# Fronts and backs for the chunks of an SSD layer, with late Tanh in the conv tiles, in a two-layer streaming encoder on one NeuronCore

## The chip, the cores and the metric

One Trainium2 chip, one of its cores. The metric is the device time of one launch, in microseconds, as a median of several runs. Where a profile is read, it is of one execution with its own time.

## The reference

Two layers over 1024 prompt frames of a new stream and 32 sample frames of a running one, width 1024, float32: a Mamba-2 SSD layer, then an HGRN2 layer, each followed by a SwiGLU feed-forward part. The change concerns the SSD layer and the very last norm. Cut to these:

```python
def ssd_mixer(h, conv_buf, ssm_state, in_w, conv_w, conv_b, dt_bias, A_log, D_skip, gnorm_w, out_w):
    proj = h @ in_w                                    # z (2048), xbc (3072), dt (32 heads)
    ...
    for tap in range(SSD_CONV_W):                      # 4 taps
        acc = acc + xpad[:, tap:tap + L].astype(jnp.float32) * conv_w[tap].astype(jnp.float32)
    xbc = jax.nn.silu(acc)                             # x (2048), B and C (4 groups x 128)
    dt = jax.nn.softplus(dt_raw.astype(jnp.float32) + dt_bias.astype(jnp.float32))
    y, S = ssd_scan(xs, dt, A, Bm, Cm, ssm_state.astype(jnp.float32))
    y = y + D_skip.astype(jnp.float32)[:, None] * xs
    yg = y.reshape(Bsz, L, SSD_D_INNER) * jax.nn.silu(z.astype(jnp.float32))
    yg = yg * lax.rsqrt(jnp.mean(yg * yg, axis=-1, keepdims=True) + NORM_EPS)   # per group of 512
    out = yg.astype(h.dtype) @ out_w

# ssd_scan, for each chunk of frames:
        y = jnp.einsum('btsg,btsgh,bsghp->btghp', cb, decay, xdt)               # inside the chunk
        y = y + jnp.einsum('btgn,bghpn->btghp', Cc, S) * jnp.exp(cum)[..., None]  # from the state
        S = jnp.exp(last)[..., None, None] * S + jnp.einsum('bsgh,bsghp,bsgn->bghpn', w_end, xdt, Bc)

# at the end of the trunk
        y = rmsnorm(x, final_norm_w)
```

## The kernel before

Features lie on the 128 partitions, frames on the free axis. The frames are worked in two halves `h`: 512 prompt frames, then 512 prompt frames and the 32 sample frames (544). Every large product is done three times in a reduced fp32 form to keep fp32 accuracy (`product`, lines L346 to L348): the weight `raw` is split by ScalarE into a high part `wh` and by VectorE into a low part `wl` (`wsplit`, recorded under the helper lines L118 and L121), and for each of 8 slices of the contraction TensorE does wh times xh, wh times xl, wl times xh. So the first L348 of a weight can't start before VectorE has made its `wl`. One tile of 128 output features takes 24 matmuls of 512 columns, or twice 24 of 256 or 272.

The SSD layer runs over eight units (half `h`, group `g` of 8 heads). A unit has six conv tiles (C and B and four of x, tile name `ca`; the products of `conv_tile` are evacuated by ScalarE as `pre`, then three taps on VectorE, a Tanh `cth` on ScalarE and a last product on VectorE), four z tiles, and chunks of 128 frames (four, in the second half also one of 32). A chunk (`ssd_chunk`) has small matmuls: scores (L620), four turns of x (L625), a turn of B (L641), the state's part of Y (L648), the new state (L651), and the chunk's own part of Y (L662). `dec`, `xdt`, `xw`, `cbm`, `ec` are made for them on ScalarE and VectorE, from the time steps `dt` (`ssd_dt`), which `ssd_cols` turns once in each half (L543), and from loads of the cumulated steps (`cumB`, `ec`), issued one chunk ahead on SP's queue. After its chunks a unit is gated: Y gets the skip term and z, the squares are summed (`sq`), a matmul adds over partitions (L369), ScalarE makes `rstd` by Ln and Exp with a table load before each, VectorE scales Y in four parts and makes the low parts `yl`. The output products of a unit (`ssd_out`), the z tiles and the next unit's conv tiles are tasks that are spread between chunks: `PRE` = 4 tasks before the first chunk, the rest evenly behind the chunks, and the conv tiles of the next unit behind the gate. In the first unit the second half's input is also squared and turned there (`x_squares`, `x_residual`, L212 and L225).

Each engine runs its own queue in order. Within it, the framework's scheduler sets the rows when the program is built, from what each instruction depends on, from buffers that come free and from where it stands in the program, so a change of the program text moves rows far from the changed lines. PSUM has five banks for products (`mm`) and three for small matmuls and sums (`sc`).

At the end of the program `last_outs` does the last eight output tiles for the first 256 frames. `finish_last` norms these frames: `first` (after tile 5) turns and squares the first four feature tiles, `second` (after tile 7) the other four, then scales and stores.

Of the kernel before, what the change touches and what calls it, by code (L numbers as in the profile page):

```python
# [11 lines left out]
AF = mybir.ActivationFunctionType  # L12
# [4 lines left out]
P = 128  # L17
# [31 lines left out]
def trunk_kernel(ctx, tc, x_prompt, x_sample, state_ssd, cache_conv, state_hgrn,  # L49
# [442 lines left out]
    def ssd_dt(h, xn, blocks, w=None):  # L492
# [4 lines left out]
        e, v, u, ln, t = [T("ys", "dt") for _ in range(5)]  # L497
# [40 lines left out]
    def ssd_cols(h):  # L538
        pk, _, elast = dts[h]
        cols = colt[:, :5 * P].rearrange("p (c t) -> p c t", t=P)  # L540
        for c, (o, n, _) in enumerate(CHUNKS[h]):
            ps = psum_sc()
            PE.transpose(ps[:n, :P], pk[:, o:o + n], ident)  # L543
            V.tensor_copy(cols[:n, c, :], ps[:n, :P])
        dts[h] = cols, elast

# [3 lines left out]
    def conv_tile(h, ct, xn, blocks, w=None):  # L550
# [60 lines left out]
    def ssd_chunk(h, g, c, S, loads, u):  # L611
        o, n, smp = CHUNKS[h][c]
        Bt, Ct, xs, Y = u["x"][0], u["x"][1], u["x"][2:], u["Y"]
        cols, elast = dts[h]
# [4 lines left out]
        ps = psum_sc()  # L619
        PE.matmul(ps[:n, :n], Bx, Cx, start=True, stop=True)  # L620
        cbm = small("cbm")
        tt(cbm[:n, :n], ps[:n, :n], cmask[:n, :n], MUL)
        ps = psum_sc()
        for j in range(4):
            PE.transpose(ps[:n, j * P:(j + 1) * P], xs[j][:, xo:xo + n], ident)  # L625
        x3 = ps[:n, :].rearrange("p (h q) -> p h q", q=64)
        xdt, xw = T("xd", "xdt")[:, :512], T("xd", "xw")[:, :512]
        tt(xdt[:n, :].rearrange("p (h q) -> p h q", q=64), x3,
           cols[:n, c, h0:h0 + 8].unsqueeze(2).to_broadcast([n, 8, 64]), MUL)
        tt(xw[:n, :].rearrange("p (h q) -> p h q", q=64), x3,  # L630
           cols[:n, c, 64 + h0:64 + h0 + 8].unsqueeze(2).to_broadcast([n, 8, 64]), MUL)
# [9 lines left out]
        PE.transpose(ps[:n, :P], Bx, ident)  # L641
# [16 lines left out]
        y1 = psum_sc()
        y13 = y1.rearrange("p (j t) -> p j t", t=P)
        for i in range(8):  # L660
            r = 64 * (i % 2)
            PE.matmul(y13[r:r + 64, i // 2, :n], xdt[:n, i * 64:(i + 1) * 64], cums[i // 4][:n, i % 4, :n],  # L662
                      start=True, stop=True)
        yo = Y[:, :, o:o + n]
        if ec is None:
            act(yo, y13[:, :, :n], AF.Copy)
        else:
            tt(yo, y13[:, :, :n], ec[:, :, :n], ADD)
# [37 lines left out]
    PRE = 4  # L706

# [3 lines left out]
    def ssd_conv_tasks(h, g, u, blocks=None, ws=()):  # L711
        order = [16 + g, 20 + g] + [4 * g + j for j in range(4)]
        ws = dict(zip(order, ws))
        return [lambda ct=ct: u["x"].append(conv_tile(h, ct, xns[h], blocks or BLK[h], ws.get(ct))) for ct in order]

    def ssd_layer(after, ws):
# [13 lines left out]
        for i, (h, g) in enumerate(units):  # L730
# [28 lines left out]
            if g == 0:  # L759
                ssd_cols(h)  # L760
# [645 lines left out]
    def finish_last(groups):  # L1406
# [20 lines left out]
        return first, second  # L1427

    def last_outs(due1, due2):
# [28 lines left out]
        first, second = finish_last(groups_of(h, 0, 256))  # L1458
# [71 lines left out]
```

## Time and profile before

| | |
|---|---|
| median of 3 runs | 2849.74 us (2848.84 to 2850.81) |
| the profiled execution | 2848.86 us, its span 2846.9 us |
| granted TensorE clock, mean | 0.999 |
| TensorE busy | 2824.4 us (99%) |
| VectorE busy | 2131.0 us (75%) |
| ScalarE busy | 1561.8 us (55%) |
| GpSimd busy | 44.5 us (2%) |
| SSD layer in the span | about 0 to 850 us |

Times in the rows are microseconds from the start of the span. In a timeline a row gives start, duration, engine, line, operation, tiles; a duration includes the filling and emptying of the engine, so neighbouring rows overlap, and what an instruction costs its queue is the difference of starts. Square brackets give the idle time of the engine ahead of a row and what ended it. In the chain of work that ended last, a row gives start, duration, line and count.

### The profile page before, as it was taken

The page shows a single profiled execution, that of the slowest core. Times are in us where ns is not written, and L with a number is a line of the kernel's source. Part 1 is how long each engine was busy: PE and PEld are TensorE (multiplying, and loading weights), DVE is VectorE, ACT ScalarE, POOL GpSimd, SP SyncE. Part 2 cuts the span into 40 slices and gives each one's busy share as a digit, 9 for nine tenths or more (in the row PEclk, how much of TensorE's full clock was granted, in tenths as well). Part 3 has the DMA queues.
Part 4 walks back from the last instruction along what each step waited for, and adds up shares of the span by engine and source line. Part 5 has one row for each costly group of instructions (what it writes and reads, how often), then busy time and mean ns, then how long its engine had stood idle before and what let it go on. Part 6 is the DMA issues. An engine that isn't in the chain of part 4 may idle for free.

```text
span 2846.9 us, 48830 instructions
## 1 busy us (share of the span) xinstructions
PE 2824.4 (99%) x19676; PEld 2609.6 (92%) x19676; DVE 2131.0 (75%) x3663; ACT 1561.8 (55%) x2846; POOL 44.5 (2%) x158
## 2 busy tenths in 40 slices
PE   8999999999999999999999999999999999999998
PEld 8777788999989999999999888999989999999998
DVE  7887887787787877797777557655668877787776
ACT  6665554564644654565544666566644554455544
POOL 0000010010000000000000000000000000000000
PEclk9999999999999999999999999999999999999999
DMA  7434344444322432333233222222232333333322
GB/s 190 115 108 115 91 109 105 115 113 106 105 83 88 126 95 91 112 89 105 90 97 105 75 74 74 76 80 80 74 89 91 113 95 92 120 97 104 110 91 69
DMA packets 394516, 281.54 MB, mean 99 GB/s; under 512 B 16289, under 2 KB 382514, under 8 KB 394290
## 3 DMA queue, kind: packets, MB, share of 16 engines
q1 hardware_dynamic: 394274, 278.42, 33.9%
q8 instruction: 154, 2.52, 0.4%
q14 instruction: 72, 0.59, 0.1%
q10 hardware_dynamic: 16, 0.00, 0.0%
HBM read 270.57 MB, written 7.82 MB: 98 GB/s over the span
## 4 chain that ended last, share of the span: by engine, by line
PE 91%; DVE 4%; ACT 2%; DMA 1%; issue 1%; SPq 0%; POOL 0%; DVEq 0%; ACTq 0%; POOLq 0%
PE mm L346 19%; PE mm L347 19%; PE mm L348 19%; PE mm L1177 5%; PE mm L1175 5%; PE mm L1176 5%; PE sc L1177 4%; PE sc L1175 4%; PE sc L1176 4%; PE sc L662 1%; PE sc L651 1%; PE sc L648 1%; PE mm L1451 1%; DVE fixed L121 1%; ACT wh L118 1%
## 5 line engine op out<-in xcount | busy, mean ns | idle before, releaser
L118 ACT ACTIVATE wh<-raw 128x512 fp32r<-128x512 f32 (+1 forms) x687 | 554.8, 816 | 592.0 <-PE mm L347 475.9
L346 PE MATMUL mm<-xn,wh 128*128 128x272 f32 (+2 forms) x1552 | 522.2, 337 | 2.0 <-ACT pre L118 2.0
L348 PE MATMUL mm<-xn,wl 128*128 128x272 f32 (+2 forms) x1552 | 515.9, 333 | 0.9 <-DVE wl L121 0.9
L347 PE MATMUL mm<-xn,wh 128*128 128x272 f32 (+2 forms) x1552 | 515.6, 333 | 0.0
L121 DVE TENSOR_TENSOR wl<-raw,wh 128x1024 fp32r<-128x1024 f32 (+1 forms) x307 | 372.9, 1217 | 144.6 <-ACT wh L118 120.4
L121 DVE TENSOR_TENSOR fixed<-mm,fixed 128x272 f32<-128x272 f32 (+3 forms) x504 | 259.2, 525 | 180.6 <-PE mm L348 173.7
L347 PE MATMUL mm<-fl,wh 128*128 128x272 f32 (+1 forms) x992 | 322.5, 326 | 0.0
L346 PE MATMUL mm<-fh,wh 128*128 128x272 f32 (+1 forms) x992 | 322.5, 326 | 0.0
L348 PE MATMUL mm<-fh,wl 128*128 128x272 f32 (+1 forms) x992 | 322.3, 325 | 0.0
L346 PEld LDWEIGHTS mm<-xn,wh 128*128 128x128 f32 x1552 | 291.4, 188 | 31.9 <-issue 3.0
L348 PEld LDWEIGHTS mm<-xn,wl 128*128 128x128 f32 x1552 | 291.6, 188 | 30.4 <-issue 1.8
L347 PEld LDWEIGHTS mm<-xn,wh 128*128 128x128 f32 x1552 | 291.9, 188 | 27.6 <-issue 1.2
L121 DVE TENSOR_TENSOR wh<-raw,wh 128x512 fp32r<-128x512 f32 x380 | 256.4, 686 | 48.5 <-ACT wh L118 45.9
L1175 PE MATMUL mm<-th,wh 128*128 128x272 f32 (+1 forms) x912 | 261.2, 286 | 0.8 <-ACT s L118 0.8
L1177 PE MATMUL mm<-th,wh 128*128 128x272 f32 (+1 forms) x912 | 260.1, 285 | 0.2 <-DVE wh L121 0.2
L1176 PE MATMUL mm<-tl,wh 128*128 128x272 f32 (+1 forms) x912 | 259.5, 285 | 0.0
L346 PEld LDWEIGHTS mm<-fh,wh 128*128 128x128 f32 x992 | 186.1, 188 | 16.0 <-ACT fh L118 1.6
L348 PEld LDWEIGHTS mm<-fh,wl 128*128 128x128 f32 x992 | 186.6, 188 | 15.4
L347 PEld LDWEIGHTS mm<-fl,wh 128*128 128x128 f32 x992 | 186.5, 188 | 14.9 <-DVE fl L121 0.2
L1175 PEld LDWEIGHTS mm<-th,wh 128*128 128x128 f32 x912 | 171.7, 188 | 2.9 <-ACT s L118 2.2
L1175 PE MATMUL sc<-xn,wh 128*128 128x272 f32 (+1 forms) x608 | 172.9, 284 | 0.5 <-ACT wh L118 0.5
L1177 PE MATMUL sc<-xn,wh 128*128 128x272 f32 (+1 forms) x608 | 173.0, 285 | 0.0
(313 smaller groups left out, 6648.8 us busy)
## 6 DMA issues: line engine op xcount, KB each, us to landing
raw<-in_ffn_w_gate_dram SPq DMA_DIRECT2D x88, 512.0 KB, 3.8
raw<-in_ffn_w_up_dram SPq DMA_DIRECT2D x88, 512.0 KB, 4.4
raw<-in_ffn_w_down_dram SPq DMA_DIRECT2D x88, 512.0 KB, 3.9
raw<-in_ssd_in_w_dram SPq DMA_DIRECT2D x80, 512.0 KB, 4.1
raw<-in_hgrn_in_w_dram SPq DMA_DIRECT2D x64, 512.0 KB, 4.3
cumB<-cumd SPq DMA_DIRECT2D x64, 256.0 KB, 4.2
raw<-in_ssd_out_w_dram SPq DMA_DIRECT2D x32, 512.0 KB, 3.5
raw<-in_hgrn_out_w_dram SPq DMA_DIRECT2D x16, 512.0 KB, 3.5
```

Of the source, the lines that this page charges most:

```text
L118: keep(A.activation(out=out, in_=in_, func=f, **kw))
L121: keep((eng or V).tensor_tensor(out=out, in0=a, in1=b, op=op))
L346: PE.matmul(ps[:, :bn], a, mh, start=(k == 0), stop=False)
L347: PE.matmul(ps[:, :bn], a, ml, start=False, stop=False)
L348: PE.matmul(ps[:, :bn], b, mh, start=False, stop=(k == n - 1))
L648: PE.matmul(y23[:, j, :n], S[:, j * P:(j + 1) * P], Cx, start=True, stop=True)
L651: PE.matmul(pp, Btok[:n, :], xw[:n, :], start=True, stop=True)
L662: PE.matmul(y13[r:r + 64, i // 2, :n], xdt[:n, i * 64:(i + 1) * 64], cums[i // 4][:n, i % 4, :n], start=True, stop=True)
L1175: PE.matmul(ps[:, :n], a, mh, start=(k == 0 and not more), stop=False, skip_group_check=True)
L1176: PE.matmul(ps[:, :n], a, ml, start=False, stop=False, skip_group_check=True)
L1177: PE.matmul(ps[:, :n], b, mh, start=False, stop=(k == 3), skip_group_check=True)
L1451: PE.matmul(ps[:, :bn], a, x[:, b0:b0 + bn], start=i == 0, stop=i == len(ts_) - 1)
```

## The change

1. `ssd_chunk` is cut into `ssd_front` (scores, the turns of B and x, and what is made of them: `cbm`, `Btok`, `xdt`, `xw`, `dec`) and `ssd_back` (the state's part of Y, the new state, the chunk's part of Y). The loop issues the back of chunk c-1, the front of chunk c, the loads of chunk c+1, then the tasks. A front takes two `mm` banks instead of `sc` banks. `LEAD` = 3 tasks stand before the first front, where `PRE` = 4 stood before the first chunk.
2. `ssd_cols` goes; the fronts of group 0 turn the time steps of their chunk themselves. One `dt` tile moves to another buffer.
3. A conv tile's Tanh and last product (`conv_silu`) are issued after the taps of the next conv tile; the last two after the last tile.
4. At the end of the program three of the four last feature tiles are turned and squared after tile 6 (`most`), the fourth after tile 7.

```diff
-        e, v, u, ln, t = [T("ys", "dt") for _ in range(5)]
+        e, v, u, ln, t = [T(k, "dt") for k in ("s", "ys", "ys", "ys", "ys")]
...
-    def ssd_cols(h):
-        pk, _, elast = dts[h]
-        cols = colt[:, :5 * P].rearrange("p (c t) -> p c t", t=P)
-        for c, (o, n, _) in enumerate(CHUNKS[h]):
-            ps = psum_sc()
-            PE.transpose(ps[:n, :P], pk[:, o:o + n], ident)
-            V.tensor_copy(cols[:n, c, :], ps[:n, :P])
-        dts[h] = cols, elast
...
+        return a, W
+
+    def conv_silu(a, W):
         th = T("w", "cth")
         act(th[:, :W], a[:, :W], AF.Tanh)
         stt(a[:, :W], th[:, :W], 1.0, a[:, :W], ADD, MUL)
-        return a
...
-    def ssd_chunk(h, g, c, S, loads, u):
+    def ssd_front(h, g, c, loads, u):
...
+        ps, px = psum_mm(), psum_mm()
         PE.matmul(ps[:n, :n], Bx, Cx, start=True, stop=True)
+        PE.transpose(ps[:n, P:2 * P], Bx, ident)
+        if not g:
+            PE.transpose(ps[:n, 2 * P:3 * P], pk[:, o:o + n], ident)
+            V.tensor_copy(cols[:n, c, :], ps[:n, 2 * P:3 * P])
+        for j in range(4):
+            PE.transpose(px[:n, j * P:(j + 1) * P], xs[j][:, xo:xo + n], ident)
+        cbm, Btok = small("cbm"), small("Btok")
         tt(cbm[:n, :n], ps[:n, :n], cmask[:n, :n], MUL)
+        act(Btok[:n, :], ps[:n, P:2 * P], AF.Copy)
...
+        return decs, ec, xdt, xw, Btok, Cx
+
+    def ssd_back(h, g, c, S, made, u):
...
         if ec is not None:
+            y2 = psum_sc().rearrange(quads, t=P)
             for j in range(4):
+                PE.matmul(y2[:, j, :n], S[:, j * P:(j + 1) * P], Cx, start=True, stop=True)
+            tt(ec[:, :, :n], y2[:, :, :n], ec[:, :, :n], MUL)
+            S3 = S.rearrange("p (h q) -> p h q", q=64)
+            tt(S3, S3, elast[:, h0:h0 + 8, c:c + 1].to_broadcast([P, 8, 64]), MUL)
+        pp, y1 = psum_sc(), psum_sc().rearrange(quads, t=P)
         PE.matmul(pp, Btok[:n, :], xw[:n, :], start=True, stop=True)
+        for i in range(8):
+            r = 64 * (i % 2)
+            PE.matmul(y1[r:r + 64, i // 2, :n], xdt[:n, i * 64:(i + 1) * 64], decs[i // 4][:n, i % 4, :n],
+                      start=True, stop=True)
...
+    LEAD = 3
...
+        made = []
+
+        def task(i, ct):
+            made.append(conv_tile(h, ct, xns[h], blocks or BLK[h], ws.get(ct)))
+            u["x"].append(made[-1][0])
+            for m in made[-2:-1] if i + 1 < len(order) else made[-2:]:
+                conv_silu(*m)
...
-            for t in tasks[:PRE]:
-                t()
-            tasks = tasks[PRE:]
-            for c, (o, n, smp) in enumerate(CHUNKS[h]):
-                nxt = chunk_loads(h, g, c + 1, False) if c + 1 < nch else None
-                ssd_chunk(h, g, c, Ss if smp else Sst[g], loads, u)
-                loads = nxt
-                q = -(-len(tasks) // (nch - c))
...
+            run(tasks[:LEAD])
+            tasks = tasks[LEAD:]
+            made = None
+            for c in range(nch + 1):
+                if c:
+                    ssd_back(h, g, c - 1, Ss if CHUNKS[h][c - 1][2] else Sst[g], made, u)
+                if c < nch:
+                    made = ssd_front(h, g, c, loads, u)
+                if c + 1 < nch:
+                    loads = chunk_loads(h, g, c + 1, False)
+                if c < nch:
+                    q = -(-len(tasks) // (nch - c))
+                    run(tasks[:q])
+                    tasks = tasks[q:]
...
+        def most():
+            for g, ss in zip(groups, sums):
+                ps, yo = psum_sc(), T("w", "yo")[:, :512]
+                turned(g, ps, range(3))
+                squared(ps, yo, 0, 384, ss[:, 1:2])
+                tt(ss[:, 0:1], ss[:, 0:1], ss[:, 1:2], ADD)
+                last.append((ps, yo))
+
         def second():
-            last = [finish_half(g, 1, ss, psum_sc, "w") for g, ss in zip(groups, sums)]
+            for g, (ps, yo) in zip(groups, last):
+                turned(g, ps, (3,))
+            for ss, (ps, yo) in zip(sums, last):
+                squared(ps, yo, 384, 512, ss[:, 1:2])
...
-        mid[5] = first
+        mid[5], mid[6] = first, most
```

How this moves rows in the queues, at three places. The numbers in names differ between the two programs.

VectorE in the first unit's conv tiles, where `wl_642` (now `wl_639`) is the low part of the fifth conv tile's weight. Before, rows 70 to 77:

```order
L121 TENSOR_TENSOR dt_361<-dt_361,dt_358 128x512
L124 SCALAR_TENSOR_TENSOR ca_350<-cth_355,ca_350 128x512
L121 TENSOR_TENSOR dt_359<-dt_359,dt_361 128x512
L121 TENSOR_TENSOR wl_642<-raw_639,wh_641 128x1024
L513 TENSOR_SCALAR dt_360<-dt_359,fixed 128x512
L517 COPY dt_358<-dt_359 32x512
L514 SCALAR_TENSOR_TENSOR dt_362<-fixed,dt_360 128x512
L124 SCALAR_TENSOR_TENSOR ca_493<-pre_438,fixed,ca_493 128x512
```

Now, rows 78 to 88, the end of rows 69 to 88:

```order
L124 SCALAR_TENSOR_TENSOR ca_350<-cth_495,ca_350 128x512
L518 COPY dt_355<-dt_359 32x512
L121 TENSOR_TENSOR dt_355<-dt_359 32x512
L528 COPY fixed<-dt_355 32x4
L124 SCALAR_TENSOR_TENSOR ca_559<-pre_504,fixed,ca_559 128x512
L124 SCALAR_TENSOR_TENSOR ca_490<-cth_564,ca_490 128x512
L121 TENSOR_TENSOR dt_355<-dt_355,dt_356 32x512
L124 SCALAR_TENSOR_TENSOR ca_559<-pre_504,fixed,ca_559 128x512
L121 TENSOR_TENSOR wl_639<-raw_636,wh_638 128x1024
L124 SCALAR_TENSOR_TENSOR ca_559<-pre_504,fixed,ca_559 128x512
L121 TENSOR_TENSOR wl_708<-raw_705,wh_707 128x1024
```

The weight moved from row 73 to row 86, behind the scan (L514, row 77 now) and the taps and last products of the tiles `ca_490` and `ca_559`.

VectorE at the first unit's gate, where the last sum of squares releases L369, and `wl_1404` (now `wl_1393`) is the low part of the weight of the next unit's fourth conv tile. Before, rows 169 to 177:

```order
L121 TENSOR_TENSOR sq_1188<-sq_1188,sq_1196 128x512
L124 SCALAR_TENSOR_TENSOR ca_1259<-pre_1230,fixed,ca_1259 128x512
L121 TENSOR_TENSOR wl_1404<-raw_1401,wh_1403 128x1024
L121 TENSOR_TENSOR wl_1463<-raw_1460,wh_1462 128x1024
L124 SCALAR_TENSOR_TENSOR ca_1259<-cth_1264,ca_1259 128x512
L124 SCALAR_TENSOR_TENSOR Y_801<-Y_801,fixed,rstd_1199 128x512 x3
L121 TENSOR_TENSOR yl_1206<-Y_801,yh_1205 128x512
L124 SCALAR_TENSOR_TENSOR Y_801<-Y_801,fixed,rstd_1199 128x512
L121 TENSOR_TENSOR yl_1211<-Y_801,yh_1210 128x512
```

Now, the sum of squares is row 173; rows 180 to 191:

```order
L225 COPY fixed<-sc_1319 128x4x128
L124 SCALAR_TENSOR_TENSOR Y_789<-Y_789,fixed,rstd_1191 128x512 x3
L121 TENSOR_TENSOR yl_1198<-Y_789,yh_1197 128x512
L124 SCALAR_TENSOR_TENSOR Y_789<-Y_789,fixed,rstd_1191 128x512
L121 TENSOR_TENSOR yl_1203<-Y_789,yh_1202 128x512
L124 SCALAR_TENSOR_TENSOR ca_1366<-pre_1337,fixed,ca_1366 128x512
L121 TENSOR_TENSOR yl_1208<-Y_789,yh_1207 128x512
L225 COPY fixed<-sc_1378 128x4x128
L121 TENSOR_TENSOR yl_1213<-Y_789,yh_1212 128x512
L121 TENSOR_TENSOR wl_1393<-raw_1390,wh_1392 128x1024
L124 SCALAR_TENSOR_TENSOR ca_1366<-cth_1430,ca_1366 128x512
L225 COPY fixed<-sc_1437 128x4x128
```

The weight moved behind the four scalings of Y and the four low parts `yl`.

TensorE at the same place. Before, from the last product ahead of L369:

```order
L347 MATMUL mm_1409<-xn,wh_1403 128x512
L369 MATMUL sc_1200<-sq_1188,fixed 128x512
L212 MATMUL sc_1271<-fixed 128x128 x4
L212 MATMUL sc_1277<-fixed 128x128 x4
L348 MATMUL mm_1409<-xn,wl_1404 128x512
L346 MATMUL mm_1409<-xn,wh_1403 128x512
```

Now:

```order
L347 MATMUL mm_1398<-xn,wh_1392 128x512
L369 MATMUL sc_1192<-sq_1180,fixed 128x512
L212 MATMUL sc_1260<-fixed 128x128 x4
L212 MATMUL sc_1266<-fixed 128x128 x4
L212 MATMUL sc_1319<-fixed 128x128 x4
L212 MATMUL sc_1325<-fixed 128x128 x4
L212 MATMUL sc_1378<-fixed 128x128 x4
L212 MATMUL sc_1384<-fixed 128x128 x4
L212 MATMUL sc_1437<-fixed 128x128 x4
L212 MATMUL sc_1443<-fixed 128x128 x4
L212 MATMUL sc_1496<-fixed,xrow_785 128x32 x4
L348 MATMUL mm_1398<-xn,wl_1393 128x512
```

All the turns of the second half's input, 36 with x4 in each row, moved in front of the L348 that needs the weight.

VectorE at the joint of the halves, where `wl_4031` (now `wl_4008`) belongs to the fourth conv tile of the second half's first unit. Before, from the scaling of Y:

```order
L124 SCALAR_TENSOR_TENSOR Y_3140<-Y_3140,fixed,rstd_3787 128x512
L121 TENSOR_TENSOR dt_3686<-dt_3686,dt_3690 128x544
L124 SCALAR_TENSOR_TENSOR ca_3876<-pre_3818,fixed,ca_3876 128x547
L121 TENSOR_TENSOR dt_3689<-dt_3689,dt_3686 128x544
L124 SCALAR_TENSOR_TENSOR ca_3876<-pre_3818,fixed,ca_3876 128x547
L121 TENSOR_TENSOR dt_3687<-dt_3687,dt_3689 128x544
L124 SCALAR_TENSOR_TENSOR ca_3876<-pre_3818,fixed,ca_3876 128x547
L121 TENSOR_TENSOR yl_3799<-Y_3140,yh_3798 128x512
L513 TENSOR_SCALAR dt_3688<-dt_3687,fixed 128x544
L517 COPY dt_3686<-dt_3687 32x544
L514 SCALAR_TENSOR_TENSOR dt_3690<-fixed,dt_3688 128x544
L121 TENSOR_TENSOR wl_4031<-raw_4028,wh_4030 128x1024
```

Now, the scaling starts at row 498; rows 503 to 514:

```order
L121 TENSOR_TENSOR yl_3784<-Y_3124,yh_3783 128x512
L121 TENSOR_TENSOR dt_3646<-dt_3650 32x512
L121 TENSOR_TENSOR dt_3646<-dt_3650 32x32
L528 COPY fixed<-dt_3646 32x4
L530 COPY fixed<-dt_3646 32x1
L124 SCALAR_TENSOR_TENSOR ca_3856<-pre_3798,fixed,ca_3856 128x547
L124 SCALAR_TENSOR_TENSOR ca_3925<-pre_3867,fixed,ca_3925 128x547
L121 TENSOR_TENSOR dt_3646<-dt_3646,dt_3647 32x544
L124 SCALAR_TENSOR_TENSOR ca_3856<-pre_3798,fixed,ca_3856 128x547
L121 TENSOR_TENSOR yl_3789<-Y_3124,yh_3788 128x512
L124 SCALAR_TENSOR_TENSOR ca_3925<-pre_3867,fixed,ca_3925 128x547
L121 TENSOR_TENSOR wl_4008<-raw_4005,wh_4007 128x1024
```

Counted from the first scaling as the first, the weight moved from row 14 to row 17, behind all of the `dt` chain and taps of two conv tiles; and on TensorE 146 products stand between the last chunk's L658 (before L662) and the L348 that needs it, where 187 stood.

More of the change, by code (lines that the diff above doesn't have):

```diff
@@ L618, in ssd_chunk @@
         cums, ec = loads
-        ps = psum_sc()
+        ps, px = psum_mm(), psum_mm()
         PE.matmul(ps[:n, :n], Bx, Cx, start=True, stop=True)
-        cbm = small("cbm")
+        PE.transpose(ps[:n, P:2 * P], Bx, ident)
[5 more added lines that the diff above has]
+        cbm, Btok = small("cbm"), small("Btok")
         tt(cbm[:n, :n], ps[:n, :n], cmask[:n, :n], MUL)
[L623 to L626, printed above, removed]
+        act(Btok[:n, :], ps[:n, P:2 * P], AF.Copy)
+        x3 = px[:n, :].rearrange("p (h q) -> p h q", q=64)
         xdt, xw = T("xd", "xdt")[:, :512], T("xd", "xw")[:, :512]
[L628 to L631, printed above, removed]
+        for t, k in ((xdt, 0), (xw, 64)):
+            tt(t[:n, :].rearrange("p (h q) -> p h q", q=64), x3,
+               cols[:n, c, k + h0:k + h0 + 8].unsqueeze(2).to_broadcast([n, 8, 64]), MUL)
+        decs = []
         for q in range(2):
@@ L644, in ssd_chunk @@
+    @lifted("chunk")
+    def ssd_back(h, g, c, S, made, u):
+        o, n, smp = CHUNKS[h][c]
+        decs, ec, xdt, xw, Btok, Cx = made
+        elast = dts[h][2]
+        h0 = g * 8
+        quads = "p (j t) -> p j t"
         if ec is not None:
-            y2 = psum_sc()
-            y23 = y2.rearrange("p (j t) -> p j t", t=P)
+            y2 = psum_sc().rearrange(quads, t=P)
             for j in range(4):
-                PE.matmul(y23[:, j, :n], S[:, j * P:(j + 1) * P], Cx, start=True, stop=True)
@@ L657, in ssd_chunk @@
             tt(S, S, pp, ADD)
[L658 to L668, printed above, removed]
+            tt(yo, y1[:, :, :n], ec[:, :, :n], ADD)
@@ L713, in ssd_conv_tasks @@
         ws = dict(zip(order, ws))
-        return [lambda ct=ct: u["x"].append(conv_tile(h, ct, xns[h], blocks or BLK[h], ws.get(ct))) for ct in order]
+        made = []
[4 more added lines that the diff above has]
+                conv_silu(*m)
+        return [lambda i=i, ct=ct: task(i, ct) for i, ct in enumerate(order)]
     def ssd_layer(after, ws):
@@ L1426, in second @@
                 finish_out(g, 1, yo)
-        return first, second
+        return first, most, second
     def last_outs(due1, due2):
@@ L1457, in last_outs @@
                 out(m, [g], 256, LEN[h] - 256)
-        first, second = finish_last(groups_of(h, 0, 256))
+        first, most, second = finish_last(groups_of(h, 0, 256))
         later = groups_of(h, 256, LEN[h])
         mid = {m: lambda g=g: finish(g) for m, g in zip((0, 2, 4), later)}
-        mid[5] = first
+        mid[5], mid[6] = first, most
         for m in range(KD):
```

27 lines of the change are left out of this document (12 added, 15 removed).

## The prediction

> **What bounds the kernel now.** I read the page's busy shares first, then the table of TensorE's waits, then the stretches around each of them.
>
> ```profile
> PE 2824.4 (99%) x19676; PEld 2609.6 (92%) x19676; DVE 2131.0 (75%) x3663; ACT 1561.8 (55%) x2846; POOL 44.5 (2%) x158
> ...
> PE mm L212 <- DMA fixed<-in_x_prompt_dram: 3.9, 1, 3.9
> PE mm L346 <- ACT pre L118: 2.0, 2, 1.5
> ...
> PE mm L348 <- DVE wl L121: 0.9, 1, 0.9
> PE sc L543 <- ACT pre L118: 0.9, 2, 0.5
> ...
> PE sc L369 <- DVE sq L121: 0.5, 1, 0.5
> ...
> 460.00:800.00 340.00, 340.00 (x2761) 321.97 (x2760) 270.93 (x439) 194.71 (x426) 19.34 (x70) 1.00 0.42 106
> ```
>
> TensorE is busy for 99% of the span. In the waits (total us, how often, longest) the SSD layer has only 2.0 + 0.9 + 0.9 + 0.5 = 4.3 us; the 3.9 is the first load and stays. The last row is a stretch of 340 us in the second half's units (columns: length, then PE, PEld, DVE, ACT, POOL busy): PE 340.00 of 340.00, DVE 271, ACT 195. So a reordering that keeps the same matmuls can win about 4.3 us, while anything that holds TensorE's queue is added in full. The question is where VectorE's new order hands TensorE an operand late.
>
> **The change, part by part.** Everything is set against the profiled execution: span 2846.9, time 2848.86, which is 0.9 us under the median of 2849.74.
>
> *Grouping of small matmuls.* As many as before: the turns of `cols` move into the fronts, the rest only stands closer together.
>
> ```profile
> 95.84 0.60 PE L625 MATMUL sc<-fixed,ca 128*128 128x128 f32 x4
> 96.20 0.48 PE L347 MATMUL mm<-xn,wh 128*128 128x512 f32 x1
> 96.52 0.27 PE L641 MATMUL sc<-fixed,ca 128*128 128x128 f32 x1
> ...
> 115.77 1.10 PE L369 MATMUL sc<-sq,fixed 128*128 128x512 f32 x2 [0.47 <-DVE sq L121]
> 116.70 1.04 PE L212 MATMUL sc<-fixed 128*128 128x128 f32 x8
> 117.50 0.48 PE L348 MATMUL mm<-xn,wl 128*128 128x512 f32 x1
> ...
> 2826.01 2.83 PE mm L1451 x24
> ```
>
> Costs are differences of starts. The last row, from the chain, gives 24 products of 256 columns in 2.83 us: 0.118 each, so 0.236 at 512 columns and 0.125 at 272. Four small ones take 0.36 us and the product behind them 0.32 instead of 0.236, 0.45 in all; eight take 0.80 and about the same exit, 0.89. Two groups of four cost what one of eight costs: grouping gives 0, within 1 us over the 36 chunks.
>
> *Steady units.* Between a front and its back stand 24 products of 512 columns or 48 of 272, 5.7 or 6.0 us, beside the rest of the chunk's matmuls; VectorE and ScalarE have room by the 340 us row. The loads of the next chunk now go behind the front on SP's queue:
>
> ```profile
> cumB<-cumd SPq DMA_DIRECT2D x64, 256.0 KB, 4.2
> ```
>
> They land 4.2 us after issue, less than those products. POOL only keeps its few memsets and carries. I take 0 here. If the cover were missing in one chunk in six, it would cost under 1 us each.
>
> *Start (30 to 64 us).* The deferred Tanh no longer stands ahead of an evacuation, which should remove this wait and one of L543:
>
> ```profile
> 39.64 1.42 DVE L121 TENSOR_TENSOR dt<-dt,dt 128x512 f32<-128x512 f32 x2 [0.74 <-ACT dt L118]
> 42.18 1.22 DVE L121 TENSOR_TENSOR wl<-raw,wh 128x1024 fp32r<-128x1024 f32 x1
> 44.05 1.21 DVE L514 TENSOR_TENSOR_SCAN dt<-fixed,dt 128x512 f32<-128x512 f32 x1
> 45.18 0.72 DVE L124 SCALAR_TENSOR_TENSOR ca<-pre,fixed,ca 128x512 f32<-128x512 f32 x1
> ...
> 51.94 0.39 PE L346 MATMUL mm<-xn,wh 128*128 128x256 f32 x1 [1.53 <-ACT pre L118]
> ```
>
> But in the new VectorE order the low part of the fifth conv tile's weight (`wl_639`) is row 86, not 73 (`wl_642`, the row at 42.18). Ahead of it stand the `dt` chain and the taps of three tiles. Row 69 waits for ScalarE's `dt`, 39.64 before; two evacuations now stand ahead of that on ScalarE, so about 41.15. Rows 69 to 86: the scan 1.13, the weight 1.13, seven tap and Tanh products at 0.66, five tensor operations at 0.6 to 0.7 and four copies and scalings at 0.2 to 0.45: 11.5 us. So `wl_639` is ready at about 52.6. TensorE reaches that tile 24 products before the wait above (50.2 - 2.8 = 47.4) and has six products that don't need it, 0.7 us. It stands 4.5 us, in two pieces; 1.53 + 0.42 go. Net **+2.5** (bounds -2, the waits gone and nothing new, and +4.5).
>
> *The first unit's gate.* Below are VectorE's and ScalarE's rows after the sum of squares that L369 waits for:
>
> ```profile
> 116.20 2.35 DVE L121 TENSOR_TENSOR wl<-raw,wh 128x1024 fp32r<-128x1024 f32 x2
> 119.91 0.69 DVE L124 SCALAR_TENSOR_TENSOR ca<-cth,ca 128x512 f32<-128x512 f32 x1 [1.35 <-ACT cth L118]
> 120.52 2.07 DVE L124 SCALAR_TENSOR_TENSOR Y<-Y,fixed,rstd 128x512 f32<-128x512 f32 x3
> 122.51 0.68 DVE L121 TENSOR_TENSOR yl<-Y,yh 128x512 fp32r<-128x512 f32 x1
> 123.11 0.74 DVE L124 SCALAR_TENSOR_TENSOR Y<-Y,fixed,rstd 128x512 f32<-128x512 f32 x1
> ...
> 117.25 0.69 ACT L118 ACTIVATE rstd<-sc,fixed 128x512 f32<-128x512 f32 x1
> 117.96 1.28 ACT L118 ACT_TABLE_LOAD   x1
> ```
>
> Before, the two weights at 116.20 come ahead of the scaling of Y, and TensorE always has conv products. Now `wl_1393` is row 189, behind all four scalings and all four `yl`. Let D be the end of the sum (row 173). ScalarE: a tap to wait for 0.66, Tanh 0.52 (a little less than Ln), a table load 1.28, Ln 0.7, a copy 0.5, a table load 1.28, Exp 0.55: scaling starts at D + 5.5. VectorE from there: four scalings and a tap at 0.66, four `yl` and a copy at 0.6, the weight at 1.17: 7.5, so D + 13.1 with the latencies. TensorE after D has L369 (0.24) and the 36 transposes of L212 at 0.10 to 0.11, held back a little by their banks: done at D + 5.0. Its next row is the L348 that needs `wl_1393`. It stands **8.1 us**. Fewer products are also left ahead of L369 than VectorE's gate takes; it waits 1.35 instead of 0.47: **+0.9**.
>
> *The joint of the halves.* The same happens to the fourth conv tile's `wl_4008` (before `wl_4031`):
>
> ```profile
> 384.93 0.69 DVE L121 TENSOR_TENSOR Y<-sc,ec 128x512 f32<-128x512 f32 x1
> ...
> 386.13 1.41 DVE L124 SCALAR_TENSOR_TENSOR Y<-ca,fixed,Y 128x512 f32<-128x512 f32 x2
> ...
> 391.19 0.69 DVE L121 TENSOR_TENSOR sq<-sq,sq 128x512 f32<-128x512 f32 x1
> ...
> 399.25 2.08 DVE L124 SCALAR_TENSOR_TENSOR Y<-Y,fixed,rstd 128x512 f32<-128x512 f32 x3 [2.10 <-ACT rstd L118]
> ...
> 409.08 1.19 DVE L121 TENSOR_TENSOR wl<-raw,wh 128x1024 fp32r<-128x1024 f32 x1
> ...
> 409.14 0.29 PE L347 MATMUL mm<-xn,wh 128*128 128x272 f32 x1
> 410.32 0.40 PE L348 MATMUL mm<-xn,wl 128*128 128x272 f32 x1 [0.90 <-DVE wl L121]
> ```
>
> Let S be the start of the last chunk's Y (384.93). Before, the weight was done at S + 25.3, and TensorE needed it at S + 24.3. Now VectorE has one weight (1.15), the gate (386.13 to 391.19, 5.06), the square sums and half the `dt` chain until S + 13.4, waits for `rstd` until S + 14.9 (L369 after 93 products of 0.125 at S + 11.6, then Ln, a table load, Exp), and has 11.4 us of rows up to `wl_4008`: S + 26.3. TensorE now has only 146 products plus L369 and four transposes behind S: it comes at S + 19.0. It stands 7.3 us. The waits of this stretch before go: the 0.90 above, and the second waits in the rows of `pre` and of L543, 2.0 - 1.5 and 0.9 - 0.4: 1.9. Net **+5.4** (bounds -1.9 and +7.3). At the six other joints the same count leaves TensorE served; the nearest has 0.3 us to spare.
>
> *The end.* Six of the eight last transposes move ahead of the last four matmuls and delay them by 0.65 us, where five were hidden; the two last squares shrink from 512 to 128 columns.
>
> ```profile
> 2838.57 0.86 PE sc L1380 x6
> ...
> 2839.45 1.27 ACT yo L118 x4
> ```
>
> Of the 0.86 some 0.65 merely moves, of the 1.27 about 0.4 goes: **+0.25** (bounds -0.4, +0.65).
>
> *The clock after a stall.* TensorE stands for longer than 3 us nowhere after the first load until its work is over. There:
>
> ```profile
> 3.00:4.00 1.00, 0.09 (x1) 0.12 (x2) 0.00 (x0) 0.20 (x1) 0.00 (x0) 1.00 0.98 281
> ...
> 2841.00:2842.00 1.00, 0.00 (x0) 0.00 (x0) 0.90 (x3) 0.85 (x2) 0.00 (x0) 1.00 0.00 0
> 2842.00:2843.00 1.00, 0.00 (x0) 0.00 (x0) 0.77 (x2) 0.72 (x1) 0.00 (x0) 0.73 0.28 104
> 2843.00:2844.00 1.00, 0.00 (x0) 0.00 (x0) 0.00 (x0) 0.00 (x0) 0.00 (x0) 0.50 1.03 393
> ```
>
> The clock granted is the third figure from the end: the last transposes end at about 2839.6, and from 2842.5 it is 0.50. After some 3 us of rest TensorE gets half its clock. How long it stays low under work no row shows; at least 0, and the longest seen is the 4.4 us to the end of the span, which would lose 2.2. I take 3 us, as long as the fall needed, so 1.5 lost, at each of the two long stalls: **+3.0** (0 to 4.4).
>
> [...]
>
> **Sum:** 2.5 + 8.1 + 0.9 + 5.4 + 0.25 + 3.0 = 20.15 us. 2848.86 + 20.15 = 2869.0, with the 0.9 to the median **2870**.
>
> **Rivals.** *The clock does not fall at the stalls* (they come in pieces, or the gate is slower under load): 2867. For it speaks the row at 3 to 4 us, where TensorE has rested 3.9 us since the start and the clock is 1.00.
>
> *The lateness is absorbed*: TensorE comes to the two places later than my count has it, because other waits or products stand before them, and VectorE is on time; the start's +2.5 and the waits that go then cancel: 2850, give or take 4. Against it: both stalls are counted from S and D, so what happens before these does not shift them. It would take 7 to 8 us of VectorE's rows to vanish.
>
> *Faster*: the deferred Tanh and the fronts remove the 4.3 us of waits in the table and cause none; at best another 1 us from grouping: 2849.7 - 5.3 = 2844.5. Its place is 50 to 62 us and 409 to 430 us, and it decides if `wl_1393` comes before D + 5.0 and `wl_4008` before S + 19.0. The 340 us row shows that nothing else is left to win.
>
> **How the numbers follow.** Stalls with the falling clock 0.50 (2870, own range 2862 to 2876), stalls without it 0.28 (2867), absorbed 0.16 (2850), faster 0.06 (2844.5). A measurement of this kernel can tell about 0.2%, 5.7 us, from no change, so slower means above 2855.4: both stall cases and the upper edge of the third, 0.80; within it 0.14; faster 0.06. The range leaves out the fast case and the lower half of the absorbed one, 0.14 together: from 2850; upwards it takes in the upper bounds of the start (2.0 more), the joint (1.9), the clock (1.4) and the end (0.4): 2870 + 5.7 = 2876.
>
> **What would show it.** In the changed kernel's waits a row of L348 on VectorE's `wl` with some 15 us in two or three waits, near 124 to 132 and near 420; a granted clock below 1.00 behind them; no L346 wait on `pre` above 1 us; the last matmul half a microsecond nearer to the end. I am wrong if those `wl` rows are short, or if the steady units show waits of TensorE.

## The result, and the profile after

The changed kernel takes 2871.86 us (median of 6 runs, 2871.07 to 2872.36), the kernel before 2849.85 beside it: a ratio of 1.0078, 95% interval [1.0068, 1.0089], 22.0 us more. 2870 was forecast. The profiled execution of the changed kernel took 2872.36 us, with a span of 2870.6 against 2846.9, so the traces differ by 23.7. Its mean granted clock is 0.995 (0.999 before).

From the page after, the span and the busy times, and then TensorE's waits (total us, how often, longest):

```profile
span 2870.6 us, 48888 instructions
...
PE 2828.4 (99%) x19676; PEld 2615.3 (91%) x19676; DVE 2125.9 (74%) x3665; ACT 1569.1 (55%) x2852; POOL 106.5 (4%) x158
```

```profile
PE mm L348 <- DVE wl L121: 17.6, 3, 8.3
...
PE mm L346 <- ACT wh L118: 3.0, 1, 3.0
PE mm L346 <- DVE fixed L121: 2.5, 3, 1.5
...
PE sc L369 <- DVE sq L121: 1.1, 1, 1.1
```

The number of matmuls is the same. The waits on `pre` and of the turned time steps are gone, and three waits for a weight's low part, 17.6 us in all, stand in their place. TensorE's timeline shows where (start, duration, line, and in brackets the idle time ahead):

```profile
52.31 0.38 PE L346 MATMUL mm<-xn,wh 128*128 128x256 f32 x1 [2.99 <-ACT wh L118]
...
54.38 0.58 PE L348 MATMUL mm<-xn,wl 128*128 128x256 f32 x1 [1.52 <-DVE wl L121]
54.76 0.41 PE L346 MATMUL mm<-xn,wh 128*128 128x256 f32 x1
54.97 0.41 PE L347 MATMUL mm<-xn,wh 128*128 128x256 f32 x1
...
123.94 1.13 PE L369 MATMUL sc<-sq,fixed 128*128 128x512 f32 x2 [1.10 <-DVE sq L121]
124.90 3.66 PE L212 MATMUL sc<-fixed 128*128 128x128 f32 x32
128.49 0.43 PE L212 MATMUL sc<-fixed,xrow 32*128 32x32 f32 x4
137.26 0.80 PE L348 MATMUL mm<-xn,wl 128*128 128x512 f32 x1 [8.35 <-DVE wl L121]
...
141.56 0.39 PE L346 MATMUL mm<-xn,wh 128*128 128x512 f32 x1
...
426.66 0.60 PE L778 MATMUL sc<-fixed,sr 128*128 128x128 f32 x4
435.00 0.59 PE L348 MATMUL mm<-xn,wl 128*128 128x272 f32 x1 [7.74 <-DVE wl L121]
...
438.47 0.29 PE L348 MATMUL mm<-xn,wl 128*128 128x272 f32 x1
```

VectorE's timeline gives the other side, the last sum of squares and the weight at the first gate, then the same at the joint of the halves:

```profile
123.20 0.68 DVE L121 TENSOR_TENSOR sq<-sq,sq 128x512 f32<-128x512 f32 x1
...
129.67 2.08 DVE L124 SCALAR_TENSOR_TENSOR Y<-Y,fixed,rstd 128x512 f32<-128x512 f32 x3 [1.40 <-ACT rstd L118]
...
136.00 1.22 DVE L121 TENSOR_TENSOR wl<-raw,wh 128x1024 fp32r<-128x1024 f32 x1
...
408.71 0.68 DVE L121 TENSOR_TENSOR Y<-sc,ec 128x512 f32<-128x512 f32 x1
...
433.73 1.22 DVE L121 TENSOR_TENSOR wl<-raw,wh 128x1024 fp32r<-128x1024 f32 x1
```

In both places VectorE works on, apart from its wait for `rstd`; the weight is simply the last of a long run of rows, while TensorE has run out of rows that can do without it.

In the stretches (length; PE, PEld, DVE, ACT, POOL busy; granted clock third from the end) the clock is at half behind all three:

```profile
53.00:59.00 6.00, 4.62 (x21) 4.62 (x22) 6.00 (x8) 1.54 (x2) 0.10 (x1) 0.50 0.92 242
...
132.00:141.00 9.00, 3.73 (x9) 2.96 (x10) 9.00 (x15) 6.24 (x12) 0.00 (x0) 0.50 0.20 63
...
432.00:438.00 6.00, 3.00 (x13) 3.00 (x14) 6.00 (x8) 4.57 (x8) 4.19 (x3) 0.50 0.80 199
...
455.00:850.00 395.00, 394.94 (x3071) 368.25 (x3070) 306.48 (x497) 218.25 (x472) 59.70 (x75) 1.00 0.40 107
```

The last row is the whole second half of the SSD layer behind the joint: TensorE rests for 0.06 us in 395, at full clock.

**Where the 23.7 us of span are.** The new waits are 17.6 + 3.0 + 1.1 = 21.7 in the table; the ones that went were 4.3, so 17.4. Counted as differences of starts it is 17.2. The clock: from 137.26 to 141.56 ten products took 4.30 us, 2.31 at their usual 0.231; from 435.00 to 438.47 fifteen took 3.47 instead of 1.88; and at the start twenty products at 0.213 instead of 0.118, with the edges, lost 2.2. Together 2.0 + 1.6 + 2.2 = 5.8. The rows without a wait, with the grouping of the small matmuls, gave back about 2.2. The wait at the entry of the first feed-forward part (the row of `fixed`, longest 1.5, before 0.5) costs 1.0, the end 0.5, and the first product starts at 15.94 instead of 14.53, 1.4 later. That makes 23.7.

### The profile page after: what moved, and what is told of

It reads as the page before. It is cut to its first block, busy times and chain, and to the rows that moved or that the text cites. A ratio compares the mean times of both kernels' runs of the same rounds, so it can differ in the third digit from the quotient of the medians.

```text
span 2870.6 us, 48888 instructions
## 1 busy us (share of the span) xinstructions
PE 2828.4 (99%) x19676; PEld 2615.3 (91%) x19676; DVE 2125.9 (74%) x3665; ACT 1569.1 (55%) x2852; POOL 106.5 (4%) x158
## 4 chain that ended last, share of the span: by engine, by line
PE 89%; DVE 5%; ACT 3%; DMA 1%; issue 1%; SPq 0%; POOL 0%; ACTq 0%; DVEq 0%; POOLq 0%
PE mm L346 19%; PE mm L348 19%; PE mm L347 19%; PE mm L1186 4%; PE mm L1184 4%; PE mm L1185 4%; PE sc L1186 3%; PE sc L1184 3%; PE sc L1185 3%; PE sc L658 1%; PE sc L655 1%; DMA raw<-in_ffn_w_up_dram 1%; DVE wh L121 1%; PE sc L650 1%; DVE fixed L121 1%
## 5 line engine op out<-in xcount | busy, mean ns | idle before, releaser
L348 PE MATMUL mm<-xn,wl 128*128 128x272 f32 (+2 forms) x1552 | 518.8, 335 | 17.7 <-DVE wl L121 17.6
L121 DVE TENSOR_TENSOR fixed<-mm,fixed 128x272 f32<-128x272 f32 (+3 forms) x540 | 268.7, 507 | 190.3 <-PE mm L348 181.0
L348 PEld LDWEIGHTS mm<-xn,wl 128*128 128x128 f32 x1552 | 293.5, 189 | 48.9 <-DVE wl L121 19.4
L348 PE MATMUL mm<-fh,wl 128*128 128x272 f32 (+1 forms) x992 | 322.8, 326 | 0.0
L348 PEld LDWEIGHTS mm<-fh,wl 128*128 128x128 f32 x992 | 186.6, 188 | 15.3
L347 PEld LDWEIGHTS mm<-fl,wh 128*128 128x128 f32 x992 | 186.6, 188 | 14.9 <-DVE fl L121 0.2
```

The source lines that it names most:

```text
L121: keep((eng or V).tensor_tensor(out=out, in0=a, in1=b, op=op))
L347: PE.matmul(ps[:, :bn], a, ml, start=False, stop=False)
L348: PE.matmul(ps[:, :bn], b, mh, start=False, stop=(k == n - 1))
```

## The experiments

My theory was that the whole loss comes from the third part, the deferred Tanh and last product: VectorE's rows are reordered by it, so that three weight splits come late, and the rests let the clock fall. The rival was that the fronts and backs bring the loss with them, because they need other banks and rows. "Ratio" is against the kernel before, timed beside it.

**Tanh at once** (label silu_at_once): all of the change but its third part.

```diff
-            for m in made[-2:-1] if i + 1 < len(order) else made[-2:]:
-                conv_silu(*m)
+            conv_silu(*made[-1])
```

> The changed kernel with its third part undone: each conv tile's Tanh and last product follow its own taps again; fronts, backs, the turned time steps and the new end stay. In its order the fifth conv tile's weight of the start is back at row 73, the first gate's weight stands again ahead of the scaling of Y, and at the joint of the halves the weight comes some 3.9 us late (7.0 by the same count in the changed kernel). Theory (late weights): the start costs nothing more than before, the first unit 1.3 us (L369 0.65, weight 0.7), the joint 3.9 + about 1.6 for a low clock - 2.8 for waits that are gone, grouping -1.7, the end +0.5: 2849.85 + 2.8 = about 2852.5 us (2850 to 2855). Rival (the cut into fronts and backs and its banks cost the time themselves): above 2865 us.

It took 2850.76, before 2850.20: ratio 1.0003 [0.9994, 1.0012]. Against the kernel before beside it, the changed kernel lost 22.0 us and this one 0.6, so some 21 of the 22 us come from the order of two instructions for each conv tile; by the interval of this run it is 19 to 24. Its stretch at the start, and the one wait on a weight that is left:

```profile
30.00:64.00 34.00, 34.00 (x275) 33.22 (x274) 27.83 (x45) 21.85 (x36) 1.63 (x10) 1.00 0.56 137
```

```profile
PE mm L348 <- DVE wl L121: 3.8, 1, 3.8
```

The stall at the joint is only halved, so the fronts and backs have a part in that one, and win about as much elsewhere. No kernel was run with the third part alone, so it stays open whether the late Tanh would cost the same in the old order.

**Deferral at the start only, and everywhere else only** (late_start, late_rest):

```diff
+            late = blocks is not None          # late_rest: blocks is None
-            for m in made[-2:-1] if i + 1 < len(order) else made[-2:]:
+            for m in (made[-2:-1] if i + 1 < len(order) else made[-2:]) if late else made[-1:]:
                 conv_silu(*m)
```

> The changed kernel with the deferred Tanh kept in the six conv tiles of the start alone; all later conv tiles have Tanh and last product behind their own taps. Theory (each place of a late weight pays for itself): the start's stalls of 3.1 and 1.7 us and some 2.4 us of low clock come back on top of silu_at_once (2850.8), less the nothing that stands there now: about 2858 us (2855.5 to 2859.5). Rival (the start's stall is absorbed by VectorE's slack in the first chunks): 2851 us.

> The complement: Tanh and last product follow their own taps in the start's six tiles, and are deferred in all later units. Theory: the stall of 8.4 us at the first gate, the 7.9 us at the joint and their low clock stay, the start's 7 us go: about 2865 us (2863 to 2867). Together with late_start the two parts make up the whole way from silu_at_once to the changed kernel, 21 us. Rival (the gate's stall comes from VectorE having fallen behind in the start): below 2860 us.

They took 2857.80 and 2863.26, before 2849.54: ratios 1.0027 [1.0017, 1.0038] and 1.0047 [1.0035, 1.0060]. Against the kernel before beside each, and less the 0.6 of silu_at_once, that is 7.7 and 13.2 us; together 20.9 of the 21.4 that lie between silu_at_once and the changed kernel. The rival of late_rest, that the gate's stall comes from VectorE having fallen behind in the start, is refuted by the 8.35 that stay there. The places add up: late_rest has two waits, 16.1 us, on the weights of the gate and the joint (8.35 and 7.78), late_start the start's 2.99 and 1.27 beside a wait of 3.83 at the joint, the one that stays with the Tanh at once. Of the 7.7 that the start costs, the stall is 4.3 and the clock 2.2.

TensorE's waits in late_start, then in late_rest:

```profile
PE mm L348 <- DVE wl L121: 5.1, 2, 3.8
...
PE mm L346 <- ACT wh L118: 3.0, 1, 3.0
```

```profile
PE mm L348 <- DVE wl L121: 16.1, 2, 8.3
```

**Weights lifted** (weights_lifted): everything as in the changed kernel, but three splits get a priority: those of the late weights of the gate and the joint, and of one more weight behind the gate. The late weight of the start gets none. In the built program the rows of three engines change around these two places, not the three splits alone.

```diff
-        w = w or wsplit(conv_w_unit(ct), KD)
+        if w is None:
+            raw = conv_w_unit(ct)
+            with tc.high_priority(100) if (h, ct) in ((0, 5), (0, 7), (1, 1)) else nullcontext():
+                w = wsplit(raw, KD)
```

> The changed kernel with all its parts; only the weight splits of three conv tiles (two in the second unit, one in the first of the second half) are given 100 rows of priority. By its order the first gate's weight is in time and the joint's 3.7 us late; the start keeps its late weight. Theory (late weights): the 8.4 us stall and its 2.0 us of low clock go, at the joint 4 us go; 2871.9 - 14.5 = about 2857 us (2854 to 2860). Rival (the deferred Tanh itself makes VectorE or ScalarE later, the weight's row is only where it shows): the stall moves to the next row and the time stays above 2866 us.

```profile
PE mm L348 <- DVE wl L121: 5.6, 3, 4.2
```

2857.82: ratio 1.0026 [1.0017, 1.0035]. The gate's stall of 8.35 is gone and the joint's 7.74 is 4.18; the start is as it was. 14 of the 22 us are won back by a priority on three splits, with the Tanh still late. This shows the mechanism for the gate and the joint: not the Tanh itself is late for anyone, but what the scheduler puts ahead of a weight because of it. For the start, only the deferral itself was taken away and put back (late_rest, late_start).

**Joint lifted** (joint_lifted): Tanh at once, and the joint's weight with priority 160.

```diff
+            with tc.high_priority(160) if (h, ct) == (1, 1) else nullcontext():
+                w = wsplit(raw, KD)
...
-                conv_silu(*m)
+            conv_silu(*made[-1])
```

> As silu_at_once, and at the joint of the halves the fourth conv tile's weight split is given 160 rows of priority, so that its low part stands ahead of the work on Y and dt. Theory (late weights): the joint's stall and its low clock go, 5.5 us less than silu_at_once: about 2847 us (2845 to 2849), 0 to 5 us faster than the kernel before. Rival (the joint is held by the dt chain or by the loads, not by this weight): within 1 us of silu_at_once.

It took 2849.77, ratio 0.9999 [0.9991, 1.0008]: within what a measurement can tell from no change, and the gain that I expected missed. It came within 1 us of silu_at_once, as the rival had it. The wait moved to another engine. TensorE's rows, then ScalarE's:

```profile
410.46 0.60 PE L780 MATMUL sc<-fixed,sr 128*128 128x128 f32 x4
413.11 0.59 PE L346 MATMUL mm<-xn,wh 128*128 128x272 f32 x1 [2.06 <-ACT Ss L118]
413.50 0.43 PE L347 MATMUL mm<-xn,wh 128*128 128x272 f32 x1
...
416.63 0.29 PE L346 MATMUL mm<-xn,wh 128*128 128x272 f32 x1
```

```profile
410.84 0.65 ACT L118 ACTIVATE dt<-dt 32x544 f32<-32x544 f32 x1 [1.94 <-DVE dt L121]
411.52 1.06 ACT L118 ACTIVATE wh<-raw 128x1024 fp32r<-128x1024 f32 x1
412.48 0.58 ACT L118 ACTIVATE Ss<-sc 128x512 f32<-128x512 f32 x1
```

The copy of the turned state `Ss` stands on ScalarE behind a row of `dt` that VectorE feeds late, and behind the weight's high part. And behind a rest of only 2.06 us the granted clock was 0.50 from 414 to 416, with products 0.227 apart instead of 0.125, until about 416.6. In the same execution the mean granted clock was also 0.83 from 490 to 500 and from 900 to 910, where it was 1.00 in that of silu_at_once: by the means 3.4 us at half clock in each. So the profiled execution kept little of the shorter stall.

**Pause filled, and joint kept busy.** Does the rest itself bring the clock down, or the stall's place? Two kernels give TensorE products whose result nobody uses, behind the four turns at the joint: 8 of 512 columns in joint_lifted (pause_filled), 24 in the changed kernel (joint_kept_busy). If the rest does, pause_filled keeps a clock of 1.00 there and ends 1.6 us earlier than joint_lifted (2849.8), at about 2848.

```diff
+                if i == 4:
+                    wm = psum_sc()
+                    for _ in range(8):
+                        PE.matmul(wm[:, :512], onesr, xns[1][0][0][:, :512], start=True, stop=True)
```

> joint_lifted with 8 products added that serve nothing (512 columns, 1.9 us), which stand right behind the four state turns, where joint_lifted rests 2.06 us and its clock falls. [...] Rival (the slow products come from the release of the wait or from the turns): 0.23 us apart for 3.4 us as in joint_lifted, 2850 us.

> The changed kernel with 24 products added that serve nothing (512 columns, into a small bank that nobody reads), 23 of them between the four state turns and the L348 that waits for the late weight of the joint, which fill 5.4 of the 7.9 us that TensorE stands there. Theory (the clock's fall is a cost of its own, caused by the rest): the weight comes at the same time as before, some 2.3 us of waiting are left, the granted clock stays at 1.00 and the products behind it start 0.125 us apart from the first; 1.6 us less than the changed kernel, which one run can't tell. Rival (the slow products behind the stall come from the stall's release, such as refilling the queue, or from the transposes): the products start 0.23 us apart for some 3 us all the same.

TensorE's rows at the joint of pause_filled, then of joint_kept_busy:

```profile
410.98 2.09 PE L785 MATMUL sc<-xn,onesr 128*128 128x512 f32 x8
413.29 0.39 PE L346 MATMUL mm<-xn,wh 128*128 128x272 f32 x1 [0.22 <-ACT Ss L118]
413.51 0.29 PE L347 MATMUL mm<-xn,wh 128*128 128x272 f32 x1
413.64 0.29 PE L348 MATMUL mm<-xn,wl 128*128 128x272 f32 x1
```

```profile
427.23 5.53 PE L783 MATMUL sc<-xn,onesr 128*128 128x512 f32 x23
435.21 0.60 PE L348 MATMUL mm<-xn,wl 128*128 128x272 f32 x1 [2.46 <-DVE wl L121]
435.60 0.43 PE L346 MATMUL mm<-xn,wh 128*128 128x272 f32 x1
435.83 0.43 PE L347 MATMUL mm<-xn,wh 128*128 128x272 f32 x1
```

In pause_filled TensorE comes to its row at about the same time (413.29 against 413.11), but with a rest of 0.22 the products are 0.125 apart at once, and the granted clock is 1.00 from 413 to 416, where it was 0.52. So the rest is the cause, as far as one profiled execution of each kernel shows it; that of pause_filled, 2845.68, is the fastest of its eleven. The kernel took 2848.57 in the median, before 2849.58: ratio 0.9997 [0.9988, 1.0006], so the 1.5 us or so are too few to be told from no change in the time; the trace tells them. In joint_kept_busy I had the stall too short: 2.46 us were left over, the clock fell (0.50 from 436 to 438), and the products are 0.227 apart as without the filling. One run of it took 2874.73, 2.9 us over the changed kernel's median. Where the 2.9 come from was not shown.

**The end alone** (most_only): the kernel before with the fourth part.

```diff
-        mid[5] = first
+        mid[5], mid[6] = first, most
```

> The kernel before with only the fourth part: three of the four last feature tiles turned and squared after tile 6. By the prediction's sum +0.25 us, by the changed kernel's trace +0.5: 2850.1 to 2850.4 us. Rival (the shorter squares at the end count in full): 2849.0 us, 0.8 less than before.

2850.31, before 2850.20: ratio 1.0001 [0.9992, 1.0010]. From the eight turns behind tile 5 to the end of the span it takes 12.68 us (12.73 in the changed kernel, 12.21 before): half a microsecond, which the runs can't show. Its first product starts at 15.77, though its start is the kernel before's; so the 1.4 us later start of the changed kernel is not of the change.

**Gate without its priority** (gate_unlifted: Tanh at once, the end as before, and the gate's rows no longer lifted; before_unlifted: the same priority taken from the kernel before).

```diff
-    HP = dict(norm=600, gate=100, hgate=0, chunk=0, hchunk=0, hchunkb=0, dt=0, wl=0, hf=0, conv=0)
+    HP = dict(norm=600, gate=0, hgate=0, chunk=0, hchunk=0, hchunkb=0, dt=0, wl=0, hf=0, conv=0)
```

> silu_at_once with the end as before (fourth part undone) and without the 100 rows of priority that the gate's work on Y has had. By its order no weight comes late at the joint (1.0 us to spare), the sum over partitions there comes 4.3 us of products later. Theory: the joint's 4.0 us stall and about 1.7 us of low clock go, the end's 0.5 too: 2850.8 - 6 = about 2845 us (2843 to 2848), faster than before by 0.1 to 0.2%. Rival (as in joint_lifted another wait takes its place, and the clock falls there): 2849 us.

> The kernel before, none of the change, only the gate's 100 rows of priority taken away as in gate_unlifted. Theory (each program text has its own rows, and a weight that comes late sets the time): by its order the third conv tile's weight at the joint comes 6.4 us late; with a low clock and less the 1.9 us of waits that go, about +6: 2856 us (2853 to 2859). Rival (the priority of the gate is a loss by itself, and gate_unlifted gained by that alone): 2846 us.

gate_unlifted took 2846.26, before 2849.54: ratio 0.9988 [0.9979, 0.9997]. Its median is the lowest of all and below both kernels; the interval lies just below 1, though the 3.3 us are less than the 0.2% taken at the outset as what can be told apart. No wait on a weight's low part is left in its table. before_unlifted took 2857.17, ratio 1.0025 [1.0015, 1.0034], with new waits:

```profile
PE mm L346 <- ACT wh L118: 3.1, 1, 3.1
PE sc L543 <- DVE dt L121: 2.7, 1, 2.7
```

The time is the one expected (2856), with the 6 us of lateness in two pieces. So the gain is not the priority's alone: the same edit costs 7.6 us in the old order and goes with the fastest kernel in the new one.

## Why the prediction was right

The likeliest case came, 22.0 us against 20.15. The mechanism was right: late weights at the three places, and a lower clock behind them. That the sum came so near is in part luck: the clock was 2.8 short and the wait at the feed-forward part's entry (1.0) was missing, while rows that I had put at nothing gave back 2.2.

- **The first gate.** Forecast: the weight at D + 13.1, TensorE there at D + 5.0, a stall of 8.1. With D = 123.8 (123.20 and a row of 0.60) the weight ends at 137.1, D + 13.3, and TensorE is idle from 128.9, D + 5.1: 8.35. The wait of L369 is 1.10, where 1.35 was forecast. Inside TensorE's 5.0 two errors cancel: L369 is two matmuls, and it takes 0.96 to the first turn behind it, not 0.24, but the 36 turns then take 4.0 and are not held back by their banks.
- **The joint.** Forecast S + 26.3 and S + 19.0, a stall of 7.3. With S = 408.71 the weight ends at 434.9, S + 26.2, and TensorE is idle from 427.3, S + 18.6: 7.74. This counting of rows from a common event is the step to copy: everything ahead of S had shifted by 23.8 us, and it did not matter. On the way two small errors cancel: the scaling of Y began at S + 14.2, not 14.9, and the rows from there took 12.0, not 11.4.
- **The start.** The stall was 2.99 + 1.52 = 4.51 in two pieces, as forecast (4.5). But both sides came later than I had them, VectorE's wait for `dt` ended at 42.63 and not 41.15, the weight at 54.24 and not 52.6. And the first piece is a wait for the high part on ScalarE, which I had not followed.
- **The clock: the term that was mis-sized.** Forecast 3.0, two stalls of 1.5; measured 5.8. For the two stalls that I had counted it is 3.6, within the bounds of 0 to 4.4: the clock was low from 131.1 to 141.4 and from 431.5 to 438.3, with products running in 4.1 and 3.3 us of it, where I took 3. The rest is a third stall. I had put the fall behind "some 3 us of rest" and counted it only for the two long stalls, and so left out the start, whose piece of 2.99 us brought the clock down too, from about 52.6 to 59.5, and lost 2.2. In joint_lifted the clock was at half behind a shorter rest still, of 2.06 us.
- **Grouping.** Forecast 0, within 1; all rows without a wait together gave back about 2.2. Between 60 and 840 us TensorE goes from small matmuls to large ones 64 times, where it was 122. The large one behind such a change costs 0.086 more, which gives 5.0 back; but the last small one ahead of it costs 0.03 where one in the middle of a group costs 0.109, which takes 4.6 again. So the grouping itself is worth 0.4; where the rest of the 2.2 comes from I did not follow.
- **Steady units.** Forecast 0: 0.06 us of rest in 395.
- **The end.** +0.25 forecast, +0.5 measured. The last product's start is 0.3 nearer to the end of the span, not half a microsecond.
- **Not in the sum.** The wait at the feed-forward part's entry, +1.0; it is in every kernel with the fronts that I ran except gate_unlifted (silu_at_once has it, at 1.7), and not in most_only, so it goes with the fronts, though not with them alone. Why its row comes late I did not follow.

Of the rivals, the clock that does not fall is refuted by the three stretches at 0.50, and the absorbed lateness by the waits. What I put forward for the first, the 1.00 in the row at 3 to 4 us, was a misreading: in the trace of before six turns of L405 from 10.28 take 1.28 us and six from 13.28 take 0.67, so TensorE began at half its rate, and the record of the clock starts only at 12.8; ahead of that the 1.00 is no measurement. The faster case was wrong for the change, but not far off for a piece of it: without the third part the rest is neutral, and with the gate's rows unlifted 3.3 us faster.

## What to carry to other kernels

Where one engine is busy for 99% of the span, an edit that keeps its work is priced by reading the new order: take an event that both queues share, count the feeding engine's rows from it to each first operand and the busy engine's rows from it to the first use, and the difference is the stall. Here that gave 8.1 and 7.3 for 8.35 and 7.74. Look at the clock behind each rest too: in the changed kernel the three places with rests of 2.99, 8.35 and 7.74 us each had a granted clock of 0.50 behind them, which cost 2.2, 2.0 and 1.6 us. And look for the late row far from the edit: two instructions moved in a conv tile made a weight late behind a gate.

## What the runs showed of the hardware

**Half the clock behind rests of 2.06 to 8.35 us.** In joint_lifted 2.06 us, 2.65 with the four turns ahead of it, had a granted clock of 0.50 behind it; 2.46 in joint_kept_busy too, and 2.99, 8.35 and 7.74 in the changed kernel; behind 0.22 in pause_filled it was 1.00. The fall did not come a fixed time after the beginning of a rest. In the changed kernel it came at 131.1 at the gate, 2.2 us after TensorE had gone idle (128.9), and at 431.5 at the joint, 4.2 after (427.3); at the start it came at 52.6, 0.32 behind the start of the product that ends the rest. In weights_lifted a rest of 4.18, from 415.9, showed in the product rate only at about 420.7; the granted clock was 1.00 from 415 to 420 and 0.50 from 421 to 424. The low clock lasted 6.8, 10.2 and 6.8 us at the changed kernel's three places, and 3.4 at the joint of joint_lifted.

At the entry of the feed-forward part the rests were shorter, in joint_lifted, then in pause_filled:

```profile
900.17 0.50 PE L346 MATMUL mm<-fh,wh 128*128 128x512 f32 x1 [1.78 <-DVE fixed L121]
```

```profile
897.25 0.50 PE L346 MATMUL mm<-fh,wh 128*128 128x512 f32 x1 [1.77 <-DVE fixed L121]
```

In joint_lifted the mean clock was 0.83 from 900 to 910; in pause_filled it was 1.00 from 890 to 910, and in silu_at_once, with a rest of 1.74 ahead of 902.21, 1.00 from 900 to 910. This is one execution of each; no limit follows from it.

**It also fell without a rest.** TensorE's rows in gate_unlifted, where the sample chunk's back and the turns of its state stand together, and the stretch behind them:

```profile
491.32 0.97 PE L650 MATMUL sc<-ca,Ss 128*128 128x32 f32 x8
492.23 1.12 PE L655 MATMUL sc<-xw,fixed 32*128 32x512 f32 x2
493.28 0.65 PE L658 MATMUL sc<-dec,xdt 32*64 32x32 f32 x16
493.86 0.66 PE L581 MATMUL sc<-fixed 128*128 128x128 f32 x4
...
494.91 0.43 PE L347 MATMUL mm<-xn,wh 128*128 128x272 f32 x1
```

```profile
495.00:498.00 3.00, 3.00 (x15) 3.00 (x15) 3.00 (x9) 2.56 (x8) 0.00 (x0) 0.50 0.42 120
```

TensorE's queue has no gap there, but for 3 us, with the clock at 1.00 from 491 to 494, it holds only matmuls of 32 rows or columns and turns, and then the products are 0.227 apart. It happened again in the same trace, behind the same rows from 597.36 to 600.31: the clock was 0.79 from 600 to 601 and 0.50 from 601 to 604. In joint_lifted, too, TensorE was busy for all of 490 to 500 while the mean clock was 0.83. It need not happen: in the changed kernel the same rows stand from 516.61 to 519.56, and the clock is 1.00 from 516 to 523. Which of the rows bring the fall, the runs don't separate; no kernel was tried with the sample chunk's back spread out.
